# Attention scores for 1024 queries at a time in a tuned single-core kernel

One change to an already tuned attention kernel is predicted without running it, then measured.

## Chip, cores, metric

One core of a Trainium2 chip. The metric is the device time of one execution in microseconds (us); the median of several runs is quoted. A ratio is the mean time of one kernel's fast runs over the mean of the other's in the same rounds, so it is not quite the ratio of the medians.

## The reference

```python
# q, k, v: (8, 2048, 512) float32
scores = np.matmul(q, k.transpose(0, 2, 1)) / np.sqrt(512)
attn_weights = special.softmax(scores, axis=-1)
return np.matmul(attn_weights, v)
```

## The kernel before

Both products, Q with K and the weights with V, use a scheme of two-by-two blocks that needs seven block products instead of eight, paid for with sums of blocks. The sums of K, Q, V and of the weights (the exponentials) are made by VectorE in 16 bits. Scores are made for `QTW` = 512 queries at a time; a matmul of the scores has 256 moving columns:

```python
    QTW = 512
    QH = QTW // 2          # 256 moving columns
    ...
    def product(self, n):  # class Group: one of the seven products, two key blocks (G = 2)
        ...
            for j in range(G):
                for c in range(2):
                    nc.tensor.matmul(
                        dst[:, j * QH:(j + 1) * QH], lhs[:, j, c, :], rhs[:, :, c, :],
                        start=(n in (1, 5) and j == 0 and c == 0), stop=(c == 1),
                        skip_group_check=True,
                    )
```

While TensorE makes the scores of one group of queries, it multiplies the weights of the group before by V, in turn: a slot is one score product, and every other slot has eight matmuls of weights and V after it.

Nothing can be reused from an earlier group at the start. So the first group's scores are made plainly (eight block products), while pieces of K, Q and V (512 rows each, K0 to K3 and so on) come in by casting loads on the GpSimd queue. The scores need K and Q transposed. In the first batch TensorE does this for all of K and for Q0 and Q1; a DMA transpose on the sync queue does it for Q2 and Q3, and for all later batches. The order of the first loads, and a small copy that holds back what follows:

```python
    load("k", 0, 1, (2, 2))
    load("k", 0, 2)
    load("k", 0, 3, room=spare[:, 0])
    load("q", 0, 1, room=spare[:, 1])
    new_v(0)
    for c in range(NCH):
        load_v(0, c)
    load("q", 0, 2, room=spare[:, 2])
    load("q", 0, 3, room=spare[:, 3])
    ...
            if what[0] == "newv":
                if g == 1:     # GpSimd reads transposed Q3: its later loads start after that
                    nc.gpsimd.tensor_copy(out=gate[:], in_=qT[0, 3][0][:, 0, 0, 0:1])
                new_v(bb)
```

The softmax here doesn't subtract the row's maximum and nothing guards it: scores larger than these inputs give would overflow.

Of the kernel before, what the change touches and what calls it, by code (L numbers as in the profile page):

```python
# [12 lines left out]
def kernel(  # L13
# [26 lines left out]
    EXP = mybir.ActivationFunctionType.Exp  # L40
    MULT = mybir.AluOpType.mult
# [4 lines left out]
    QTW = 512  # L46
    NQS = QTW // P
    NQT = T // QTW
# [4 lines left out]
    QH = QTW // 2  # L53
    VP = D + 8
    TP = H + 8
    inv_sqrt_d = float(1.0 / np.sqrt(D))

    G = 2
    NG = NJ // G
    COPY = mybir.ActivationFunctionType.Copy  # L60

    const = ctx.enter_context(tc.tile_pool(name="const", bufs=1))
    stage = ctx.enter_context(tc.tile_pool(name="stage", bufs=4))
    kpool = ctx.enter_context(tc.tile_pool(name="kpool", bufs=5))
    qpool = ctx.enter_context(tc.tile_pool(name="qpool", bufs=3))
    vpool = ctx.enter_context(tc.tile_pool(name="vpool", bufs=2))
    ppool = ctx.enter_context(tc.tile_pool(name="ppool", bufs=2))
    opool = ctx.enter_context(tc.tile_pool(name="opool", bufs=4))
# [18 lines left out]
    qT, kT = {}, {}  # L87
    staged = {}
    vs = {}
# [33 lines left out]
    def operands(what):  # L123
        pool = kpool if what == "k" else qpool
        raw = pool.tile([P, CH, ND, P], F16, tag=what + "raw")
        sums = [pool.tile([P, 2, 2, P], F16, tag=what + f"s{n}", name=what + f"s{n}") for n in (1, 2, 4)]
        return [raw] + sums

    def dma_transpose(what, b, c):
        src = staged.pop((what, b, c))  # L130
        t = operands(what)
        nc.sync.dma_start_transpose(
            out=t[0][:].rearrange("p n c r -> p (n c) r"),
            in_=src[:].rearrange("p n d -> p (n d)"),
        )
        (kT if what == "k" else qT)[b, c] = t

    def transposed(what, b, c, n, src, w, copy):
        if n == 0:
            (kT if what == "k" else qT)[b, c] = operands(what)  # L140
        t = (kT if what == "k" else qT)[b, c]
        tr = psum["px"].tile([P, 2, ND, P], F16, tag="px", name="tr")
        for m in range(w):
            for dc in range(ND):
                nc.tensor.transpose(  # L145
                    tr[:, m, dc, :], src[:, n + m, dc * P:(dc + 1) * P], ident[:]
                )
        copy(out=t[0][:, n:n + w], in_=tr[:, 0:w])

    def pe_transpose(what, b, c, n0=0, n1=CH):  # L150
        src = staged[what, b, c]
        for n in range(n0, n1, 2):
            transposed(what, b, c, n, src, 2, nc.scalar.copy if n else nc.vector.tensor_copy)
        if n1 == CH:
            staged.pop((what, b, c))

    def first_transpose(what, n):
        transposed(what, 0, 0, n, staged[what, 0, 0], 1, nc.vector.tensor_copy)

    def k_blocks(t):  # L160
        w = t[0][:].rearrange("p (j s) c r -> p j s c r", s=2)
        return w[:, :, 0, 0:2], w[:, :, 0, 2:4], w[:, :, 1, 0:2], w[:, :, 1, 2:4]

    def q_blocks(t):
        w = t[0]
        return w[:, 0:2, 0:2], w[:, 2:4, 0:2], w[:, 0:2, 2:4], w[:, 2:4, 2:4]
# [3 lines left out]
    def k_sums(b, c):  # L170
        t = kT[b, c]
        a11, a12, a21, a22 = k_blocks(t)
        _, s1, s2, s4 = t
# [7 lines left out]
    def q_sums(b, c):  # L181
        t = qT[b, c]
        b11, b12, b21, b22 = q_blocks(t)
        _, t1, t2, t4 = t
        return [
            lambda: sub(t1[:], b12, b11),
            lambda: sub(b12, b22, b12),  # L187
            lambda: sub(t2[:], b22, t1[:]),
            lambda: sub(t4[:], b21, t2[:]),
        ]  # L190

    def new_v(b):
        vh = vpool.tile([P, NJ, 2, VP], F16, tag="vh")
        t1 = vpool.tile([P, NJ, TP], F16, tag="t1")
        t2 = vpool.tile([P, NJ, H], F16, tag="t2")
        t4 = vpool.tile([P, NJ, H], F16, tag="t4")
        nc.gpsimd.memset(vh[:, :, 1, D:D + 1], 1.0)
        nc.gpsimd.memset(t1[:, :, H:H + 1], 1.0)
        vs[b] = (vh, t1, t2, t4)

    def load_v(b, c):
        dst = vs[b][0][:].rearrange("p j s d -> p (j s) d")
# [3 lines left out]
    def v_sums(b, c):  # L206
        vh, t1, t2, t4 = vs[b]
# [4 lines left out]
            lambda: sub(t1[:, js, 0:H], b12, b11),  # L212
            lambda: sub(b12, b22, b12),
            lambda: sub(t2[:, js], b22, t1[:, js, 0:H]),
            lambda: sub(t4[:, js], b21, t2[:, js]),  # L215
        ]

    def new_p(g):
        left = [ppool.tile([P, NJ, QH], F16, tag=f"left{s}", name=f"left{s}") for s in range(2)]
        right = ppool.tile([P, NJ, 2, QH], F16, tag="right")  # L220
        sums = [ppool.tile([P, NJ, QH], F16, tag=f"s{n}", name=f"s{n}") for n in (1, 2, 4)]
        pts[g] = (left, right, sums)
# [4 lines left out]
    def plain_tile(g, kb):  # L227

        b, qt = divmod(g, NQT)
        if kb == 0:  # L230
            new_p(g)
        st = bank("qz" if kb % 3 == 2 else "qx")
        c, n = divmod(kb, CH)
        for dc in range(ND):
            nc.tensor.matmul(  # L235
                st[:], kT[b, c][0][:, n, dc, :], qT[b, qt][0][:, :, dc, :],
                start=(dc == 0), stop=(dc == ND - 1),
            )
        left, right, _ = pts[g]
        exp(left[kb % 2][:, kb // 2, :], st[:, 0:QH])  # L240
        exp(right[:, kb // 2, kb % 2, :], st[:, QH:QTW])

    def plain_half(g, j, half):

        b, qt = divmod(g, NQT)
        if j == 0 and half == 0:
            new_p(g)
        st = bank("qx")
        kt, qt_ = kT[b, j // G][0], qT[b, qt][0]
        for s in range(2):  # L250
            for dc in range(ND):
                nc.tensor.matmul(
                    st[:, s * QH:(s + 1) * QH], kt[:, 2 * (j % G) + s, dc, :],
                    qt_[:, 2 * half:2 * half + 2, dc, :],
                    start=(s == 0 and dc == 0), stop=(dc == ND - 1), skip_group_check=True,
                )
        left, right, _ = pts[g]
        if half:
            exp(right[:, j], st[:].rearrange("p (s q) -> p s q", s=2))
        else:  # L260
            for s in range(2):
                exp(left[s][:, j, :], st[:, s * QH:(s + 1) * QH])

    class Group:


        def __init__(self, g, n):
            self.g, self.n = g, n
            self.js = slice(n * G, (n + 1) * G)
            b, qt = divmod(g, NQT)  # L270
            self.a, self.b = kT[b, n], qT[b, qt]

        def product(self, n):
            a11, a12, a21, a22 = k_blocks(self.a)
            b11, b12, b21, b22 = q_blocks(self.b)
            _, s1, s2, s4 = self.a
            _, t1, t2, t4 = self.b
            if n == 1:
                if self.n == 0:
                    new_p(self.g)  # L280
                self.left, self.right, _ = pts[self.g]
# [13 lines left out]
            for j in range(G):  # L295
                for c in range(2):
                    nc.tensor.matmul(  # L297
                        dst[:, j * QH:(j + 1) * QH], lhs[:, j, c, :], rhs[:, :, c, :],
                        start=(n in (1, 5) and j == 0 and c == 0), stop=(c == 1),
                        skip_group_check=True,  # L300
                    )
            getattr(self, f"after{n}", lambda: None)()

        def two(self, t):
            return t[:].rearrange("p (j q) -> p j q", j=G)

# [5 lines left out]
        def after5(self):  # L312
            self.cz = czpool.tile([P, G, 2, QH], F32, tag="cz")
            nc.scalar.copy(out=self.cz[:, :, 1, :], in_=self.two(self.z))  # L314

        def after6(self):
            nc.scalar.copy(out=self.cz[:, :, 0, :], in_=self.two(self.x))  # L317

        def after7(self):
            nc.vector.tensor_add(self.cz[:, :, 1, :], self.two(self.x), self.cz[:, :, 1, :])  # L320

        def after3(self):
            nc.vector.tensor_add(self.cz[:, :, 0, :], self.two(self.z), self.cz[:, :, 0, :])  # L323

        def after4(self):
            exp(self.left[1][:, self.js, :], self.two(self.x))

        def after2(self):
            exp(self.left[0][:, self.js, :], self.two(self.y))

        def exp_right(self):
            exp(self.right[:, self.js], self.cz[:])

    def p_sums(g, n):
        left, right, (s1, s2, s4) = pts[g]
        js = slice(n * G, (n + 1) * G)
        a11, a21 = left[0][:, js], right[:, js, 0]
        a12, a22 = left[1][:, js], right[:, js, 1]
# [6 lines left out]

    class Pair:
# [3 lines left out]
        def __init__(self, g, i):  # L350
            self.g, self.i, self.done = g, i, 0

        def product(self, n):
            g, i = self.g, self.i
            left, right, (s1, s2, s4) = pts[g]
            vh, t1, t2, t4 = vs[g // NQT]
            cols = slice(i * P, (i + 1) * P)
            self.apart = g == NP - 1 and i == 1
            own = "q" if self.apart else "p"
# [4 lines left out]
            elif n == 5:  # L364
# [4 lines left out]
                3: (lambda j: s4[:, j, cols], lambda j: vh[:, j, 1, H:D + 1], "z"),  # L369
                4: (lambda j: right[:, j, 1, cols], lambda j: t4[:, j, :], "x"),  # L370
                5: (lambda j: s1[:, j, cols], lambda j: t1[:, j, 0:H + 1], "z"),
                6: (lambda j: s2[:, j, cols], lambda j: t2[:, j, :], "x"),
# [22 lines left out]
        def store(self, o, half, ds=slice(0, D)):  # L395
            b, qt = divmod(self.g, NQT)
# [273 lines left out]
```

## Time and profile before

| | before |
|---|---|
| median of 3 runs | 806.75 us (806.2 to 807.15) |
| span of the profiled run | 805.1 us |
| TensorE matmuls / weight loads busy | 99% / 88% |
| VectorE / ScalarE busy | 73% / 71% |
| granted TensorE clock | 1.0 throughout |

The prediction shows the lines behind this table and reads them. Matmuls overlap in the trace, so their cost is read from start to start, not from their drawn length.

These are the DMA issues between 0 and 70 us (what, queue, operation and count, then the median from issue to landing in us):

```profile
raw<-vh SPq DMA_TRANSPOSE x2, 4.6
raw<-stage SPq DMA_TRANSPOSE x1, 10.1
```

The two transposes of the first batch landed 4.4 and 4.8 us after their issue (4.6 is the median). The third, at 60 us, took 10.1.

### The profile page before, as it was taken

The page shows a single profiled execution, that of the slowest core. Times are in us where ns is not written, and L with a number is a line of the kernel's source. Part 1 is how long each engine was busy: PE and PEld are TensorE (multiplying, and loading weights), DVE is VectorE, ACT ScalarE, POOL GpSimd, SP SyncE. Part 2 cuts the span into 40 slices and gives each one's busy share as a digit, 9 for nine tenths or more (in the row PEclk, how much of TensorE's full clock was granted, in tenths as well). Part 3 has the DMA queues.
Part 4 walks back from the last instruction along what each step waited for, and adds up shares of the span by engine and source line. Part 5 has one row for each costly group of instructions (what it writes and reads, how often), then busy time and mean ns, then how long its engine had stood idle before and what let it go on. Part 6 is the DMA issues. An engine that isn't in the chain of part 4 may idle for free.

```text
span 805.1 us, 18445 instructions
## 1 busy us (share of the span) xinstructions
PE 798.2 (99%) x7244; PEld 705.1 (88%) x7244; DVE 591.4 (73%) x1477; ACT 571.1 (71%) x1039; POOL 72.7 (9%) x117
## 2 busy tenths in 40 slices
PE   8999999999999999999999999999999999999998
PEld 5788888888888888888888888888888888888887
DVE  4977787787767778677777777777777777766653
ACT  5767767767767777677677677677777776776773
POOL 4020103000030000300002000110002001000000
PEclk9999999999999999999999999999999999999999
DMA  9999966989379992998829997299972998921112
GB/s 207 202 182 179 166 129 116 209 151 183 92 125 216 153 173 70 155 219 142 154 79 162 208 152 154 64 183 197 172 142 67 189 198 158 156 69 46 54 40 79
DMA packets 190246, 116.56 MB, mean 145 GB/s; under 512 B 124496, under 2 KB 172880, under 8 KB 190160
## 3 DMA queue, kind: packets, MB, share of 16 engines
q0 software_dynamic: 49648, 49.29, 39.5%
q1 hardware_dynamic: 140368, 66.08, 39.3%
q8 instruction: 56, 0.92, 0.5%
q14 instruction: 30, 0.25, 0.1%
q10 hardware_dynamic: 144, 0.03, 0.0%
HBM read 100.70 MB, written 33.55 MB: 167 GB/s over the span
## 4 chain that ended last, share of the span: by engine, by line
PE 96%; DVE 2%; DMA 2%; POOL 0%; ACT 0%; issue 0%; SPq 0%; DVEq 0%
PE t L380 48%; PE t L297 46%; DMA stage<-in_k_dram 1%; PE t L235 1%; DMA first<-in_q_dram 1%; PE tr L145 0%; POOL stage L107 0%; DVE t L215 0%; DVE o L391 0%; DVE cz L323 0%; DVE right L342 0%; DVE s L340 0%; ACT o L388 0%; DVE raw L187 0%; DVE s L341 0%
## 5 line engine op out<-in xcount | busy, mean ns | idle before, releaser
L297 PEld LDWEIGHTS <-raw 128*128 128x128 f16 x1984 | 194.1, 98 | 23.4 <-issue 0.6
L388 ACT ACTIVATE o<-t,r 128x256 f32<-128x256 f32 x256 | 122.5, 478 | 128.6 <-DVE r L408 105.7
L297 PE MATMUL t<-raw 128*128 128x256 f16 x1488 | 203.0, 273 | 0.0
L225 ACT ACTIVATE left<-t 128x512 f16<-128x512 f32 (+1 forms) x264 | 156.8, 595 | 21.4 <-PE t L297 18.9
L380 PEld LDWEIGHTS <-s 128*128 128x128 f16 x1536 | 150.3, 98 | 18.5 <-issue 0.2
L297 PEld LDWEIGHTS <-ks 128*128 128x128 f16 x1488 | 145.6, 98 | 17.9 <-issue 0.8
L391 DVE SCALAR_TENSOR_TENSOR o<-t,r,o 128x256 f32<-128x256 f32 x192 | 92.4, 482 | 81.3 <-PE t L380 48.3
L297 PE MATMUL t<-qs,ks 128*128 128x256 f16 x992 | 139.0, 273 | 0.5 <-ACT t L310 0.4
L225 ACT ACTIVATE right<-cz 128x1024 f16<-128x1024 f32 x124 | 132.7, 1070 | 1.5 <-DVE cz L320 1.5
L380 PE MATMUL t<-t,s 128*128 128x257 f16 (+1 forms) x1024 | 133.1, 273 | 0.0
L380 PE MATMUL t<-vh,left 128*128 128x256 f16 x1024 | 132.7, 273 | 0.0
L314 ACT COPY cz<-t 128x512 f32<-128x512 f32 x124 | 72.8, 587 | 67.3 <-PE t L297 67.3
L380 PEld LDWEIGHTS <-right 128*128 128x128 f16 x1024 | 100.2, 98 | 12.2 <-issue 0.6
L320 DVE TENSOR_TENSOR cz<-t,cz 128x512 f32<-128x512 f32 x124 | 85.2, 687 | 34.6 <-PE t L297 34.6
L380 PEld LDWEIGHTS <-left 128*128 128x128 f16 x1024 | 100.2, 98 | 11.6
L323 DVE TENSOR_TENSOR cz<-t,cz 128x512 f32<-128x512 f32 x124 | 84.8, 684 | 1.9 <-PE t L297 1.9
L297 PE MATMUL t<-qs,raw 128*128 128x256 f16 x496 | 74.4, 273 | 0.5 <-DVE cz L320 0.5
L297 PE MATMUL t<-raw,ks 128*128 128x256 f16 x496 | 74.4, 273 | 0.0
L340 DVE TENSOR_TENSOR s<-right 128x512 f16<-128x512 f16 x128 | 54.0, 422 | 27.2 <-ACT right L225 22.2
L317 ACT COPY cz<-t 128x512 f32<-128x512 f32 x124 | 73.2, 591 | 0.2 <-PE t L297 0.2
L310 ACT COPY t<-t 128x512 f32<-128x512 f32 x124 | 70.7, 570 | 3.3 <-ACT o L388 0.3
L380 PE MATMUL t<-vh,s 128*128 128x257 f16 x512 | 66.7, 273 | 0.0
(51 smaller groups left out, 614.1 us busy)
## 6 DMA issues: line engine op xcount, KB each, us to landing
out_dram<-o SPq DMA_DIRECT2D x127, 256.0 KB, 2.8
vh<-in_v_dram POOLq DMA_DIRECT2D x32, 512.0 KB, 14.9
stage<-in_k_dram POOLq DMA_DIRECT2D x29, 512.0 KB, 8.5
stage<-in_q_dram POOLq DMA_DIRECT2D x28, 512.0 KB, 10.3
vh<-in_q_dram POOLq DMA_DIRECT2D x3, 512.0 KB, 20.3
raw<-stage SPq DMA_TRANSPOSE x56, 6.5
first<-in_q_dram SPq DMA_DIRECT2D x2, 256.0 KB, 3.6
first<-in_k_dram SPq DMA_DIRECT2D x2, 256.0 KB, 3.8
```

Of the source, the lines that this page charges most:

```text
L225: nc.scalar.activation(out=out_, in_=in_, func=EXP, scale=inv_sqrt_d)
L235: nc.tensor.matmul(st[:], kT[b, c][0][:, n, dc, :], qT[b, qt][0][:, :, dc, :], start=(dc == 0), stop=(dc == ND - 1),)
L297: nc.tensor.matmul(dst[:, j * QH:(j + 1) * QH], lhs[:, j, c, :], rhs[:, :, c, :], start=(n in (1, 5) and j == 0 and c == 0), stop=(c == 1) ...
L310: nc.scalar.copy(out=self.y[:], in_=self.x[:])
L314: nc.scalar.copy(out=self.cz[:, :, 1, :], in_=self.two(self.z))
L317: nc.scalar.copy(out=self.cz[:, :, 0, :], in_=self.two(self.x))
L320: nc.vector.tensor_add(self.cz[:, :, 1, :], self.two(self.x), self.cz[:, :, 1, :])
L323: nc.vector.tensor_add(self.cz[:, :, 0, :], self.two(self.z), self.cz[:, :, 0, :])
L340: lambda: add(s1[:, js], a21, a22),
L380: nc.tensor.matmul(dst[:, 0:width], lhs(j), rhs(j), start=(first and j == 0), stop=(j == NJ - 1), skip_group_check=True,)
L388: nc.scalar.activation(out=out_, in_=src, func=COPY, scale=r[:])
L391: nc.vector.scalar_tensor_tensor(out=out_, in0=src, scalar=r[:], in1=out_, op0=MULT, op1=ADD)
```

## The change

The intent is fewer and wider matmuls, and less room and work for sums. Scores are made for 1024 queries together, with 512 moving columns. The sums of the weights are made for 128 query pairs when needed, 1024 elements at a time. One fixed set of sums serves K, Q and V instead of rotating buffers. The first plain group is now 1024 queries long, so K3 is wanted some 10 us later (at 33.5 us instead of about 23.5). K3, Q2 and Q3 now go by DMA transpose; V is loaded last; the gate is gone.

```diff
-    QTW = 512
+    QH = 512
+    QW = 2 * QH
 ...
-            for j in range(G):
-                for c in range(2):
-                    nc.tensor.matmul(
-                        dst[:, j * QH:(j + 1) * QH], lhs[:, j, c, :], rhs[:, :, c, :],
+            for dc in range(2):
+                nc.tensor.matmul(
+                    dst[:], lhs[:, j, dc, :], rhs[:, :, dc, :],
 ...
-    kpool = ctx.enter_context(tc.tile_pool(name="kpool", bufs=5))
-    qpool = ctx.enter_context(tc.tile_pool(name="qpool", bufs=3))
-    vpool = ctx.enter_context(tc.tile_pool(name="vpool", bufs=2))
+    spool = ctx.enter_context(tc.tile_pool(name="spool", bufs=2))
 ...   (fixed tiles kraw, ks, qraw, qs, vh, vt1, vt2, vt4)
-            if what[0] == "newv":
-                if g == 1:
-                    nc.gpsimd.tensor_copy(out=gate[:], in_=qT[0, 3][0][:, 0, 0, 0:1])
-                new_v(bb)
 ...
     load("k", 0, 1, (2, 2))
-    load("k", 0, 2)
-    load("k", 0, 3, room=spare[:, 0])
-    load("q", 0, 1, room=spare[:, 1])
-    ...
+    load("q", 0, 1, room=spare[:, 0])
 ...
+    load("k", 0, 2)
+    load("k", 0, 3, room=spare[:, 1])
+    load("q", 0, 2, room=spare[:, 2])
+    load("q", 0, 3, room=spare[:, 3])
+    for c in range(NCH):
+        load_v(0, c)
+    plain_quarter(1, 0)
+    pe_transpose("k", 1, 0, 2)
+    plain_quarter(1, 1)
+    dma_transpose("k", 0, 3)
+    dma_transpose("q", 0, 2)
+    dma_transpose("q", 0, 3)
```

## The prediction

> **What bounds the kernel now.** I read the page first (busy shares, the row of the granted clock, the chain), then the windows of the steady part, then what TensorE itself waits for, then the chain of the first 60 us in order of time, and last the groups of VectorE by form. Page, parts 1, 2 and 4:
>
> ```profile
> PE 798.2 (99%) x7244; PEld 705.1 (88%) x7244; DVE 591.4 (73%) x1477; ACT 571.1 (71%) x1039; POOL 72.7 (9%) x117
> ...
> PEclk9999999999999999999999999999999999999999
> ...
> PE 96%; DVE 2%; DMA 2%; POOL 0%; ACT 0%; issue 0%; SPq 0%; DVEq 0%
> ```
>
> Full clock throughout, and 96% of the chain is TensorE, so the question is how far apart matmuls start, not how long each is drawn in the trace. Windows of the steady part look alike (window, length, busy time and count of PE, PEld, DVE, ACT, POOL, then clock and DMA):
>
> ```profile
> 100.00:200.00 100.00, 100.00 (x918) 89.54 (x916) 77.73 (x195) 72.42 (x131) 9.06 (x14) 1.00 0.88 157
> 600.00:700.00 100.00, 100.00 (x917) 89.54 (x916) 75.80 (x190) 72.74 (x133) 9.82 (x15) 1.00 0.92 158
> ```
>
> The chain gives the spacing from start to start (start, length, what), of the 512-column form in the first two lines, and of the 256-column form in the others:
>
> ```profile
> 17.55 3.45 PE t L235 x16
> ...
> 21.89 2.59 PE t L235 x12
> ...
> 36.68 1.31 PE t L297 x12
> ...
> 129.53 0.88 PE t L380 x8
> 141.77 0.88 PE t L380 x8
> 154.01 0.88 PE t L380 x8
> ```
>
> 512 columns: 3.45/16 = 215.6 ns and 2.59/12 = 215.8, so 215.7. 256 columns: 1.31/12 = 109.2. The last three lines lie 12.24 us apart, half a group of queries, which holds 56 score and 56 weight matmuls (16 of them of 257 columns): 12.24/112 = 109.3, the same. The slope is (215.7 - 109.2)/256 = 0.416 ns a column, which leaves 2.7 ns fixed per matmul. The waits of TensorE in the whole run:
>
> ```profile
> PE t L548 <- DVE warm L512: 1.2, 1, 1.2
> PE t L297 <- DVE cz L320: 0.5, 1, 0.5
> PE t L297 <- ACT t L310: 0.4, 1, 0.4
> ```
>
> The list has three more, of 0.2 to 0.3 us, all in the first 17 us. From 60 us to 780 us TensorE never waits. What is lost lies at the two ends. Windows of TensorE alone (length, busy, count, clock, DMA):
>
> ```profile
> 27.79:40.00 12.21, 11.76 (x104) 1.00 1.23 200
> 40.00:60.00 20.00, 19.41 (x177) 1.00 0.97 181
> 60.00:80.00 20.00, 20.00 (x186) 1.00 1.05 174
> ```
>
> A full 20 us counts 186 (matmuls cut by an edge count too); 40 to 60 us lacks 9 and the stretch before it 10, together about 2 us.
>
> **What the Trainium skill says.** "TensorE: Matmul & The Clock Gate", section "Wait — 56ns, not 53.3ns?": a warm matmul of N columns takes N/2.4 ns plus a fixed 2.5 ns or so, 215.7 ns at 512 columns. The trace agrees: 215.7, and 2.7 fixed. The same page, section "Back-to-back issue gap", gives a sustained 131 ns for 512 columns; 215.7 in this trace contradicts it, and I use the trace. Had it been true, the change would be worth 1680 x 0.085 = 140 us more.
> "Perfetto Trace Analysis", section "Identifying the Most-Contended Engine", says to judge by weight-load busy time instead of matmul busy time. Weight loads are 88% busy at 98 ns each, under the 109.2 ns of a matmul, and nothing waits for them; so fewer loads bring nothing by themselves here.
> "VectorE: DVE Perf Modes", section "The perf-mode tier table", has tensor_tensor on 16-bit data in SBUF at two elements a cycle. The f16 sums of 512 elements here take 0.42 us, spaced 0.33 to 0.34 us in the chain. 512 elements more would cost 512/2/0.96 = 267 ns (an estimate from that page), so a sum of 1024 is about 0.69 us, spaced 0.60.
>
> **The change part by part.** Counts are from listing both kernels' instructions; both build, and the changed one is free of races.
> - Score products (seven instead of eight): 3472 matmuls of 256 columns become 1680 of 512. 1680 x 0.2157 = 362.4 us against 3472 x 0.1092 = 379.1: -16.7 us. (Their columns fall by 28,672, because the first block, made the plain way, is now 1024 queries instead of 512.)
> - Plain scores at the start: 112 matmuls of 512 instead of 48 (the 32 of 256 stay): +64 x 0.2157 = +13.8 us.
> - TensorE transposes at the start: 80 instead of 96; sixteen took 0.89 us in the chain: -0.9 us. The sixteen that are gone (K's last piece of the first batch) go by DMA.
> - Products of weights and V: 2560 + 1024 matmuls in both kernels: 0.
> Sum on TensorE: -16.7 + 13.8 - 0.9 = -3.8 us. As a check: 2048 columns more (+0.85 us) and 1744 matmuls fewer at 2.7 ns (-4.7 us) give the same.
> - VectorE: sums of weights 512 of 512 elements become 192 of 1024, 64 of 768 and 64 of 256; Q sums 124 of 512 become 60 of 1024; score additions 248 become 240 at 0.69 us. By the durations above: 512 x 0.42 - (192 x 0.69 + 64 x 0.56 + 64 x 0.29) = 28, 124 x 0.42 - 60 x 0.69 = 11, and 5 us: busy 591 to about 548. ScalarE: 12 copies at 0.58 and some exponentials fewer, 571 to about 562. Neither is on the path, so worth nothing directly.
> - Weight loads: 5500 instead of 7244, 88% to 67% busy. Worth nothing either.
> - Single sums of K, Q and V: each must be rewritten between its last use and its first use in the next batch. K and Q have four slots or more (a slot is one score product, plus eight weight products in every other: 0.43 or 1.31 us). V is tight: 16 sums of 512 stand in 21 slots at the head of each batch.
>
> **The tight place, by hand.** In those 21 slots TensorE needs 21 x 0.431 + 10 x 0.873 = 17.8 us. VectorE has there, at the spacing in the trace: 16 V sums x 0.34 = 5.4; 6 score additions x 0.60 = 3.6; weight sums 6 x 0.60 + 4 x 0.21 = 4.4; one Q sum 0.6; five output additions x 0.40 and the reciprocals = 2.3. Together 16.3 us, 92%. Following the order of the queue, the V sums end about when their products want them: the last ones of the in-place difference and of the last sum have from none to -0.2 us of slack. I put 0 to 0.3 us a batch, seven batches: 0.7 us.
>
> **The start.** The loads of the first batch land one after the other, 2.65 us a piece (page: about 205 GB/s), K1 at 13.8, V3 at 32 us, well before V's first use at 32.1 (no wait was shown). The changed kernel puts V last: ten pieces end at 37.5, plus three DMA transposes that take about 2.25 us of transfer each (two and one load took 7.1 us at the end of the first phase), so V3 lands at 42 to 44.5. The plain phase ends at 13.8 + 24.2 + 2.2 (transposes) + 0.5 = 40.7, and V is wanted three to four us later: about 0 to 1 us of wait. Against that, VectorE is less crowded there, so some of the 2 us that are lost before 60 us should come back. I take 0 for the two together, plus or minus 1.5.
>
> Total: 806.75 - 3.8 + 0.7 + 0 = 803.65, say 803.7 us.
>
> **Rivals.**
> - Wide matmuls hide weight loads better and so gain much. For: 88% busy loads. Against: a spacing that the columns explain to 2.7 ns, with no waits. It would make 660 to 790 us; 1%.
> - VectorE becomes the bound at the head of each batch. For: 92% in that stretch, where the weight sums are longer and block the additions that free score banks. Against: 73% on average, falling to 68%. At 1 us a batch it makes 810; at 3 us, 824.
> - Transfers: single buffers delay the loads of K, transposes wait on the last reader, and the queue of the stores stands behind them; four output buffers would then hold up ScalarE. For: three staging buffers instead of four, and DMA 80 to 100% busy already. Against: K and Q sums are wanted five us or more after I estimate them in place. It would make 806 to 815.
> - The first phase waits longer for V or Q: 806 to 809.
>
> **Range and chances.** The arithmetic part is sure to some 0.3 us; the waits can hardly fall by over 2 us and can grow by 4. So 801.2 to 808.0. Over 2% faster would be below 790.6, less than the columns allow: 1%. Over 2% slower would be above 822.9, half a us lost in each of 32 query groups: 3%. Within 2%: 96%.
>
> **What would show it.** The matmul count 7244 to 5500, with 512-column matmuls 215.7 apart; TensorE still 98 to 99% busy; weight loads near 67%, VectorE near 548 us; the waits of TensorE short, those for V sums or weight sums at most 0.3 us at each batch head; plain scores ending near 41 us. Wrong would be a steady window whose columns do not fill its time, or a first phase over 2 us longer than reckoned.

## The result, and the profile after

The changed kernel took 820.68 us (818.58 to 821.16, 4 runs) against 806.68 us for the kernel before in the same rounds: ratio 1.017, 95% interval 1.015 to 1.019. The time is above the predicted range (801.2 to 808.0), and in the wrong direction. By the 2% mark it counts as the same; the loss of 14 us is nonetheless clear of noise.

The page, parts 1 and 2:

```profile
PE 799.8 (98%) x5500; PEld 536.0 (66%) x5500; DVE 547.1 (67%) x1212; ACT 570.9 (70%) x1020; POOL 71.6 (9%) x103
...
PEclk9979999999999999999999999999999999999999
```

Counts and busy times are as predicted (5500 matmuls, weight loads 67%, VectorE 548 us); only ScalarE, put at 562, is off. What was not expected is the 7 in the clock row, in the third slice of 20 us. The three longest waits of TensorE for what another engine or a transfer had to finish:

```profile
PE t L227 <- DMA kraw<-vh: 5.8, 1, 5.8
PE t L278 <- DMA qraw<-vh: 2.0, 1, 2.0
PE t L278 <- DVE qs L191: 2.0, 1, 2.0
```

All three are new: K3 transposed, Q2 transposed, then the first sum of Q, which needs Q3 transposed. Where they fall and what the clock does, by windows (length, busy and count of PE, clock, DMA):

```profile
36.00:39.00 3.00, 0.00 (x0) 0.90 1.22 196
39.00:42.00 3.00, 2.77 (x7) 0.50 1.22 197
42.00:45.00 3.00, 3.00 (x8) 0.50 1.48 163
45.00:48.00 3.00, 3.00 (x14) 0.96 1.11 178
...
54.00:57.00 3.00, 3.00 (x9) 0.50 0.99 132
57.00:60.00 3.00, 3.00 (x17) 0.68 1.17 184
60.00:63.00 3.00, 2.87 (x20) 1.00 0.55 90
```

With each spell of waiting the clock goes to half for about 7 us; PE looks fully busy and does half the matmuls (8 of 512 columns in 3 us, not 14). The timeline of TensorE gives the sizes (start, length, what):

```profile
39.23 10.04 PE L227 MATMUL t<-qraw,kraw 128*128 128x512 f16 x32 [5.78 <-DMA kraw<-vh]
51.27 0.60 PE L278 MATMUL t<-qraw,kraw 128*128 128x512 f16 x2 [2.00 <-DMA qraw<-vh]
53.86 1.89 PE L278 MATMUL t<-qs,ks 128*128 128x512 f16 x4 [1.99 <-DVE qs L191]
...
60.53 0.59 PE L278 MATMUL t<-qraw,kraw 128*128 128x512 f16 x2
```

From 39.23 to 51.27 us stand 32 plain matmuls and a wait of 2.0; at 215.7 ns the matmuls need 6.9 of these 12.0 us: 3.1 us lost. From 51.27 to 60.53 us stand 12 matmuls of 512 and 16 of 256 columns, 4.3 us of work, in 9.3 us, of which 2.0 are the wait: 2.9 us lost. With the waits, 5.8 + 2.0 + 2.0 + 3.1 + 2.9 = 15.8 us. The profiled run took 818.58 us; less 15.8 that is 802.8, and the prediction without its V term was 803.0. So nearly the whole miss lies before 60 us, and the rest of the kernel does what was reckoned. (The profiled run is the fastest of the four. The median lies 2.1 us above it, and no kept trace shows where.) The chain in the steady part confirms it, first before, then after:

```profile
125.17 0.87 PE t L297 x8
126.04 0.87 PE t L380 x8
```

```profile
125.23 0.86 PE t L278 x4
126.09 0.87 PE t L373 x8
```

Four score matmuls of 512 columns replace eight of 256, at 0.86 us instead of 0.87.

Why did the transposes land so late? DMA issues of the first 60 us (median from issue to landing):

```profile
qraw<-vh SPq DMA_TRANSPOSE x2, 19.2
kraw<-vh SPq DMA_TRANSPOSE x1, 18.1
```

K3 took 18.1 us, where those of the first batch took 4.4 and 4.8 in the kernel before. The 19.2 is the median of two unlike times: Q2 took 27.6 us and Q3 10.7. All three are issued in turn on the sync queue, and the chain of the first 70 us (start, length, what) shows it:

```profile
23.62 18.60 SPq L143
...
42.31 10.71 DMA qraw<-vh
...
53.11 0.70 DVE qs L191
```

The instruction that issues Q2's transpose lasted 18.6 us, past the landing of K3 (39.2 us), so Q3's was issued at 42.3 only. Q2 landed at 51.2 and Q3 at 53.0, 1.8 us apart, once the loads had run out at 50.7. So the crowd holds each transpose, and the queue puts them one behind the other. The packet records of the trace, counted for each 5 us over the 16 engines of transfer (starts; mean time of a packet on its engine):

```
from us   load packets, 1 KB landing   transpose packets, 256 B
20        1007, 98 ns                  none
25         768, 96 ns                  753, 31 ns
30         759, 96 ns                  786, 31 ns
35         767, 96 ns                  754, 31 ns
```

One to one: it looks as if an engine takes one packet of each queue in turn, so that a transpose packet of 31 ns waits for a load packet of 96. A transpose has 2048 packets, 128 for each engine: 128 x (96 + 31) ns = 16.3 us, the figure that the expectations below use. Packets overlap in the trace, however, as matmuls do. The counts give one transpose packet in about 105 ns on each engine; K3's went from 25.0 to 38.3 us, 13.3 us, and 3.9 us passed between the issue and the first packet. So 16.3 comes near the 18.1 only because two errors partly cancel. Nearly alone, the 2048 packets need 2.0 to 2.7 us (kernel before and e1_gate_v); the kernel before started its transposes at 34.6 us when only the load of Q3 was left.

The Trainium skill has this rule: "DMA: Bandwidth & Descriptors", section "Queues, rings and completion order", says that each transfer engine goes round the queues it has work for, packet by packet. The trace agrees in the counts (753 to 786 of each in 5 us). The page's packet is a group of descriptors, though, and whether a record of the trace is such a group is not shown. The page was not consulted before the prediction.

**Theory.** The loss comes from the crowd in the first 50 us: three DMA transposes, one behind the other, beside up to seven loads (four of V, and three of the second batch, which nothing holds back now). **Rivals:** the transposes are slow whatever runs beside them; the low clock is a loss of its own; the waits add up one by one; the steady part (V sums, single buffers) loses too.

### The profile page after: what moved, and what is told of

It is laid out like the page before. It is cut to its first block, busy times and chain, and to the rows that moved or that the text cites. A ratio compares the mean times of both kernels' runs of the same rounds, so it can differ in the third digit from the quotient of the medians.

```text
span 816.4 us, 14479 instructions
## 1 busy us (share of the span) xinstructions
PE 799.8 (98%) x5500; PEld 536.0 (66%) x5500; DVE 547.1 (67%) x1212; ACT 570.9 (70%) x1020; POOL 71.6 (9%) x103
## 4 chain that ended last, share of the span: by engine, by line
PE 92%; DMA 3%; SPq 2%; DVE 1%; ACT 0%; POOL 0%; issue 0%; DVEq 0%
PE t L373 48%; PE t L278 44%; SPq L143 2%; DMA vh<-in_q_dram 2%; DMA qraw<-vh 1%; DMA first<-in_k_dram 1%; DVE vt L208 0%; SPq L128 0%; ACT o L381 0%; POOL stage L118 0%; POOL vh L118 0%; DVE qs L191 0%; DVE qs L192 0%; DVE cz L301 0%; PE tr L153 0%
## 5 line engine op out<-in xcount | busy, mean ns | idle before, releaser
L278 PE MATMUL t<-qraw,kraw 128*128 128x512 f16 x720 | 195.1, 380 | 2.0 <-DMA qraw<-vh 2.0
L384 DVE SCALAR_TENSOR_TENSOR o<-t,r,o 128x256 f32<-128x256 f32 x192 | 92.3, 481 | 108.6 <-PE t L373 50.7
L278 PEld LDWEIGHTS <-kraw 128*128 128x128 f16 x960 | 94.0, 98 | 64.8 <-DMA qraw<-vh 2.5
L278 PE MATMUL t<-qs,ks 128*128 128x512 f16 x480 | 133.8, 381 | 2.0 <-DVE qs L191 2.0
L373 PE MATMUL t<-vt,s 128*128 128x257 f16 (+1 forms) x1024 | 133.2, 273 | 0.1
L220 ACT ACTIVATE right<-cz 128x1024 f16<-128x1024 f32 x120 | 127.3, 1061 | 1.1 <-DVE cz L298 1.1
L292 ACT COPY cz<-t 128x512 f32<-128x512 f32 x120 | 70.3, 586 | 75.0 <-PE t L278 74.5
L278 PEld LDWEIGHTS <-ks 128*128 128x128 f16 x720 | 70.5, 98 | 49.8 <-DVE qs L191 2.5
L278 PE MATMUL t<-qraw,ks 128*128 128x512 f16 x240 | 71.8, 381 | 0.0
L278 PE MATMUL t<-qs,kraw 128*128 128x512 f16 x240 | 71.4, 379 | 0.0
L295 ACT COPY cz<-t 128x512 f32<-128x512 f32 x120 | 69.8, 582 | 0.3 <-PE t L278 0.3
L373 PE MATMUL t<-vt,right 128*128 128x256 f16 x512 | 67.2, 272 | 0.0
## 6 DMA issues: line engine op xcount, KB each, us to landing
vh<-in_v_dram POOLq DMA_DIRECT2D x32, 512.0 KB, 10.7
```

Of the source, the lines that this page charges most:

```text
L220: nc.scalar.activation(out=out_, in_=in_, func=EXP, scale=inv_sqrt_d)
L278: nc.tensor.matmul(dst[:], lhs[:, j, dc, :], rhs[:, :, dc, :], start=(n in (1, 5) and dc == 0), stop=(dc == 1), skip_group_check=True,)
L292: nc.scalar.copy(out=self.cz[:, 1, :], in_=self.z[:])
L295: nc.scalar.copy(out=self.cz[:, 0, :], in_=self.x[:])
L373: nc.tensor.matmul(dst[:, 0:width], lhs(j), rhs(j), start=(first and j == 0), stop=(j == NJ - 1), skip_group_check=True,)
L384: nc.vector.scalar_tensor_tensor(out=out_, in0=src, scalar=r[:], in1=out_, op0=MULT, op1=ADD)
```

## The experiments

Each is the changed kernel with the edit shown, unless said otherwise. The kernel before ran in the same rounds: 807.2 us in the first four experiments, 807.3 in the next four, 807.6 in the last two. The changed kernel's 820.68 is from its own rounds (with 806.68 beside it), so differences from it carry about 0.6 us of that drift. All ten gave correct results.

### e2_pe_all: no DMA transposes in the first batch

```diff
-    dma_transpose("k", 0, 3)
-    dma_transpose("q", 0, 2)
-    dma_transpose("q", 0, 3)
 ...
+        if (kb, half) == (9, 1):
+            pe_transpose("k", 3)
+        if (kb, half) == (11, 1):
+            pe_transpose("q", 2)
+        if (kb, half) == (12, 1):
+            pe_transpose("q", 3)
```

> The changed kernel with the three DMA transposes of the first batch done on TensorE instead (48 transposes of 128x128 at 55.6 ns, 2.7 us more of TensorE). Theory (crowding): no wait for kraw or qraw is left, the clock stays full, and the time is the arithmetic sum of the prediction without its V term, 803.0, plus 2.7: 805 to 807 us. Rival (the loss comes from the steady part, from V sums or the single buffers): the time stays above 815 us.

Measured: 806.14 us (805.82 to 806.68), ratio to before 0.999 (0.998 to 1.000). Its waits of TensorE, but for the 1.2 us at the very start that all these kernels have:

```profile
PE tr L153 <- DVE qraw L156: 0.5, 2, 0.3
PE t L240 <- DVE kraw L156: 0.4, 1, 0.4
PE t L278 <- ACT t L288: 0.3, 1, 0.3
```

That is all, and the clock is 1.0. The 14 us are gone although every steady part of the change is still there, single sums of V included. The rival of the steady part falls, and the arithmetic (803.0 + 2.7 = 805.7) holds to half a microsecond. Against the kernel before the time is the same within the noise.

### e1_gate_v: V's loads wait for the transposes

```diff
-    for c in range(NCH):
-        load_v(0, c)
     plain_quarter(1, 0)
 ...
     dma_transpose("q", 0, 3)
+    nc.gpsimd.tensor_copy(out=gate[:], in_=raw_of("q", 0, 3)[:, 0, 0, 0:1])
+    for c in range(NCH):
+        load_v(0, c)
```

> The changed kernel with the loads of V (and everything after them on that queue) held back until the third DMA transpose of the first batch has landed. Theory (crowding): in the changed kernel the three transposes share the 16 transfer engines with up to seven queued loads, packet for packet, so each takes 16 us and more, and TensorE waits 5.8 + 2.0 + 2.0 us and loses its full clock. With the loads held, the transposes land by about 34 us (some 5 us or less for each once the Q loads are in), the wait for kraw is gone, V lands at about 45 us and costs a new wait of some 2 us before the first weight product: 804 to 807 us in all. Rival (a transpose is slow whatever runs beside it, or three in a row are): the waits for kraw and qraw stay near 6 and 4 us and the time stays near 820 or grows.

Measured: 812.39 us (810.52 to 814.58), ratio 1.007. The DMA issues and the waits of TensorE:

```profile
qraw<-vh SPq DMA_TRANSPOSE x2, 5.4
kraw<-vh SPq DMA_TRANSPOSE x1, 7.2
```

```profile
PE t L373 <- DMA vh<-in_v_dram: 4.5, 3, 2.1
```

The transposes land in 7.2 (K3), 6.5 and 4.3 us (5.4 is the median of these two), and the waits for them are gone. So neither one alone nor three in a row are slow in themselves. The time missed its range: V's last piece arrived at 48.9 us, not 45, since the loads restarted only after a pause; TensorE waited 0.5, 2.1 and 1.9 us in a row, and here too the clock was at half for about 7 us, from 45.6 us.

### e5_gate_next: only the second batch's loads wait

```diff
     dma_transpose("q", 0, 3)
+    nc.gpsimd.tensor_copy(out=gate[:], in_=raw_of("q", 0, 3)[:, 0, 0, 0:1])
```

> The changed kernel with only the loads of the second batch held until the third DMA transpose has landed, as a gate did in the kernel before; the V loads stay where they are. Theory (turns by packet): at 25 us some 1950 load packets are left instead of 3486, 122 for each engine, so the crowd ends at about 40.5 us instead of 50; the first transpose still lands near 39 us and TensorE still waits 5 to 6 us for it, but the other two land at about 46 us instead of 53, before the plain scores end, so the two waits of 2.0 us go: the time falls by 4 to 6 us against the changed kernel, to 815 to 817 us. Rival (V's loads alone are enough crowd): it falls by less than 2 us.

Measured: 813.35 us (811.1 to 813.87), ratio 1.007: 7.3 us less than the changed kernel (8.3 by the two ratios; either is uncertain by some 2 us). The range, 815 to 817, was missed on the good side. The first transpose still landed at 41 us, and the others in time:

```profile
PE t L227 <- DMA kraw<-vh: 6.4, 1, 6.4
...
PE t L278 <- DVE vt L208: 0.3, 1, 0.3
```

So one line, such as the change dropped, accounts for some 7 us. Most of what remains is the wait for K3 beside V's loads, 6.4 us and a spell of half clock after it.

### e4_halves: load packets of half the size

```diff
-        nc.gpsimd.dma_start(out=dst[:, ns, 0:D], in_=srcs["v"][b, :, ns, :])
+        for ds in (slice(0, H), slice(H, D)) if b == 0 else (slice(0, D),):
+            nc.gpsimd.dma_start(out=dst[:, ns, ds], in_=srcs["v"][b, :, ns, ds])
 ...   (the same for the loads of K and Q of the second batch)
```

> The changed kernel with the first batch's V loads and the second batch's loads cut in two by columns, so that each load packet has half the bytes and there are twice as many. Theory (the engines take one packet of each queue in turn; 768 load and 753 to 786 transpose packets were counted in each 5 us from 25 to 40 us): a transpose packet then waits for a load packet of some 50 to 60 ns instead of 96, so the first transpose takes about 128 x 90 ns = 11 us instead of 16, lands near 34 us, the kraw wait falls from 5.8 us to under 2, and the time falls by 4 to 9 us. Rival (the transposes get what is left in bytes, or are held by their own issue on the sync queue): the landing of the first transpose and the time do not move by more than 1 us, or get worse.

Measured: 816.91 us (816.67 to 819.33), ratio 1.013. The packets per 5 us:

```
from us   load packets, 512 B landing   transpose packets, 256 B
30        1179, 59 ns                   1225, 31 ns
35        1193, 59 ns                   1190, 31 ns
```

K3's landing, from the DMA issues, and the wait for it:

```profile
kraw<-vh SPq DMA_TRANSPOSE x1, 13.8
...
PE t L229 <- DMA kraw<-vh: 2.4, 1, 2.4
```

Still one to one, and the transpose's rate rises by 1.6 although the loads move fewer bytes (0.61 MB in 5 us instead of 0.78). K3 landed 13.8 us after its issue instead of 18.1 (4.0 us to its first packet, then 8.7 for 2048 packets, instead of 3.9 and 13.3), and its wait fell from 5.8 to 2.4 us; under 2 was expected. Equal turns by packet are shown, for two sizes of load packet. A split by bytes is not what these counts look like; nor is a fixed pace of the issuing queue, which follows the crowd: the issue of Q2 lasted 11.5 us here, 18.6 in the changed kernel and 5.0 in e1_gate_v. The time fell by 3.8 us only, below the expected 4 to 9: with twice as many load packets the crowd lasts longer (Q3 landed at 54.2 us), and TensorE waited 8.3 us for the Q sum that needs Q3. These waits are those of the profiled run, 819.33, the slowest of the four.

### e8_k3_pe: only K3 on TensorE

```diff
-    dma_transpose("k", 0, 3)
 ...
+        if (kb, half) == (11, 1):
+            pe_transpose("k", 3)
```

> The changed kernel with only K's last piece of the first batch transposed on TensorE; the two Q pieces stay with DMA. The 5.8 us wait for kraw must vanish. Theory (the phase ends when the last of the crowded transposes lands; the waits and the slow clock before that are not additive): with one transpose fewer the last Q piece lands near 47 to 51 us, TensorE waits 6 to 10 us there instead, and the time falls by 3 to 6 us only, to 815 to 818 us. Rival (waits add up): the time falls by the 5.8 us and the 3.0 us of slow clock after it, 8 to 9 us, less 0.9 us of transposes, to 812.5 to 813.5 us.

Measured: 816.21 us (815.64 to 816.49), ratio 1.011: 4.5 us less, within the theory's range. The 5.8 us wait is gone and another has taken its place:

```profile
PE t L278 <- DVE qs L191: 8.8, 1, 8.8
```

The waits do not add up. The start ends when the last crowded transpose (Q3) has landed; taking away an earlier wait moves the waiting to Q3.

### e3_fill: dummy matmuls in the waits

```diff
+        if (kb, half) == (12, 0):
+            idle(26)
         plain_tile(kb, half, "qz" if n % 3 == 2 else "qx")
 ...
     while background:
         background.popleft()()
+    idle(32)
```

> The changed kernel with 26 and 32 dummy matmuls of 512 columns where TensorE waits in the first 60 us; the waits' causes are left as they are. Theory: of the 15 us lost, about 6 us (3.0 in the last 32 plain matmuls, 3.1 after them) are not waiting but matmuls at the lower clock that the granted-clock row shows after the first wait; with the wait filled the clock stays at 1.0 and the time falls by 5 to 7 us, to 813 to 816 us. Rival (the clock loss is hidden under the later waits for qraw and its sums, which end when the transposes land, 51 to 53 us, whatever the clock): only the part after 53 us comes back, the time falls by 2 to 4 us, to 816.5 to 818.5.

Measured: 818.91 us (817.85 to 819.89), ratio 1.015: only 1.8 us less, a smaller gain than either expected, and nearer the rival's. The clock did stay up:

```profile
40.00:60.00 20.00, 18.57 (x90) 1.00 1.19 182
```

So idling causes the low clock. What the clock costs by itself stays open: 1.8 us came back, of about 6 lost at half clock. The 3.1 us before the waits for Q2 and Q3 lie under those waits, which end when the transposes land. Part of the rest was eaten by the filler itself (the last dummies ran until 54.97 us, later than the 53.86 at which the changed kernel got its Q sum), and TensorE then waited 1.5 us for a sum of V, the next thing in line.

### e10_split: the width alone undone

From e2_pe_all, each score matmul cut in two:

```diff
-            for dc in range(2):
-                nc.tensor.matmul(
-                    dst[:], lhs[:, j, dc, :], rhs[:, :, dc, :],
-                    start=(n in (1, 5) and dc == 0), stop=(dc == 1),
+            for h in range(2):
+                for dc in range(2):
+                    nc.tensor.matmul(
+                        dst[:, h * 256:(h + 1) * 256], lhs[:, j, dc, :], rhs[:, 2 * h:2 * h + 2, dc, :],
+                        start=(n in (1, 5) and h == 0 and dc == 0), stop=(dc == 1),
```

> The version with all first-batch transposes on TensorE (806.1 us), with every score matmul of 512 columns cut into two of 256: the width of the change alone is undone, all else stays. Theory of the prediction (2.7 ns fixed per matmul, weight loads hidden): 1680 matmuls more, 1680 x (2 x 109.2 - 215.7) = 4.5 us slower, 810 to 811.5 us. Rival (width is worth nothing): within 1 us. Rival (the wide form also hides weight loads or waits): slower by over 8 us.

Measured: 810.26 us (809.33 to 812.5), ratio 1.0038 (1.0024 to 1.0052), against 0.9990 for e2_pe_all. The difference of the ratios is 0.48%, 3.9 us, uncertain by some 1.5; 4.5 were reckoned. That is what 512 columns are worth here: a fixed few nanoseconds on 1680 matmuls. TensorE was as free of waits as before (0.3 us at most after 17 us), so no wait and no weight load was hidden by the width.

### e6_one_dma: one transpose back on DMA

From e2_pe_all, with Q3 loaded before K3 and transposed by DMA:

```diff
+    load("q", 0, 3, room=spare[:, 3])
     load("k", 0, 3, room=spare[:, 1])
     load("q", 0, 2, room=spare[:, 2])
-    load("q", 0, 3, room=spare[:, 3])
 ...
+    dma_transpose("q", 0, 3)
 ...
-        if (kb, half) == (12, 1):
-            pe_transpose("q", 3)
```

> A try for a version that beats both: all first-batch transposes on TensorE but the last Q piece's, which goes by DMA and whose load is moved ahead of K's last and Q's third piece. By turns of packets that single transpose takes 128 x 127 ns = 16.3 us beside the loads, from about 22 to 38.5 us, before it is wanted at about 42 us. So no wait, and 16 x 55.6 ns = 0.9 us less than with all on TensorE: 804.5 to 806 us, 0.1 to 0.3% under the kernel before. Rival: it lands after 42 us and costs 1 us or more of wait: 807 us or more.

Measured: 806.94 us (805.8 to 808.92, 6 runs), ratio 0.9993 (0.998 to 1.0007): the range was missed. The transpose landed 18.8 us after its issue at 20.0 us, in time, as the turns by packet say, but the median shows nothing of the 0.9 us saved and lies 1.6 us above the sum. Its profiled run, the fastest at 805.8, had a new wait, of 1.0 us, on ScalarE (whose output tile also waits for a store). Why the runs spread over 3 us is not settled. One source of spread shows in the twelve kept traces: the first score matmul of 512 columns, which waits for the first loads, starts between 12.85 us (this run) and 15.38 us (e10_split), although those loads are nearly the same in all.

### e9_best and e2b_again: a version from the findings

Q2 and Q3 load before K3 and go by DMA transpose with V held back (as in e1_gate_v), K3 goes through TensorE, and the first weight product stands four slots later:

```diff
-    load("k", 0, 3, room=spare[:, 1])
     load("q", 0, 2, room=spare[:, 2])
     load("q", 0, 3, room=spare[:, 3])
-    for c in range(NCH):
-        load_v(0, c)
+    load("k", 0, 3, room=spare[:, 1])
 ...
-    dma_transpose("k", 0, 3)
     dma_transpose("q", 0, 2)
     dma_transpose("q", 0, 3)
+    nc.gpsimd.tensor_copy(out=gate[:], in_=raw_of("q", 0, 3)[:, 0, 0, 0:1])
+    for c in range(NCH):
+        load_v(0, c)
 ...
+        if (kb, half) == (11, 1):
+            pe_transpose("k", 3)
 ...
-        return {2 * n + (5 if g == 0 else 1): x for n, x in enumerate(order)}
+        if g == 0:
+            return dict(zip([9, 11, 13, 16, 17, 18, 19, 21, 23, 25, 26, 27], FIRST))
+        return {2 * n + 1: x for n, x in enumerate(order)}
```

> A version built on the findings: the two Q pieces load before K's last piece and go by DMA transpose with the V loads held until they have landed (so nearly alone on the engines), K's last piece goes through TensorE (16 transposes, 0.9 us), and the first weight product stands four slots (1.7 us) later. Theory: the Q transposes land near 31 to 33 us, V's last piece near 45 us, the first weight product wants it at 45.6 us, no wait is left, and the time is 803.0 + 0.9 = 803.9, that is 803.5 to 805.5 us, 0.2 to 0.4% under the kernel before. Rival: V lands late as in the run with held V loads (48.9 us there), a wait of 2 to 4 us and a spell of low clock: 807 to 810 us.

> The version with all first-batch transposes on TensorE once more, beside the one above on the same chip: 805.5 to 807 us, 0.0 to 0.2% under the kernel before, and 1 to 2 us over the version above if that one has no waits.

Measured: e9_best 804.88 us (803.86 to 806.12), ratio 0.9968 (0.9954 to 0.9982); e2b_again 806.26 us, ratio 0.9984 (0.9972 to 0.9997); before 807.56 us. Both are in their ranges. The transposes of e9_best, and its two longest waits past the start:

```profile
qraw<-vh SPq DMA_TRANSPOSE x2, 6.8
```

```profile
PE t L278 <- DVE cz L298: 0.5, 1, 0.5
PE t L278 <- DVE vt L208: 0.3, 1, 0.3
```

This version beats both kernels, the one before by 0.3%, 2.7 us. That is about what the sums give once the start is in order (-3.8 + 0.9 = -2.9 us).

## Why the prediction was wrong

- **The width.** The -3.8 us on TensorE was right, as far as these runs can tell. Reckoned from the kernel before in the same rounds, e2_pe_all, e2b_again, e9_best and e10_split all land within 0.5 us of sums built on it (e2_pe_all: 807.2 - 3.8 + 2.7 = 806.1, measured 806.14); e6_one_dma lies 1.6 us above its sum. For K3's move to DMA the prediction counted the 0.9 us that TensorE saves and not what it then waits for.
- **The steady part.** The 0.7 us for V sums were not spent; in e2_pe_all TensorE waits for nothing between 60 us and the last stretch. The rival of VectorE was rightly held unlikely.
- **The start: the step that failed.** The prediction took "three DMA transposes that take about 2.25 us of transfer each", from two transposes that ran nearly alone in the kernel before, and used it only to place V; it never set the landing of K3, Q2 and Q3 against the time at which TensorE wants them. The 2.25 us are right for a transpose alone. Beside queued loads the packets of one took 13.3 us, and its landing came 18 to 19 us after the issue (K3, and the first transpose of e3_fill, e5_gate_next, e6_one_dma and e8_k3_pe), because the engines serve the two queues in equal turns, and the transposes follow one another on theirs. K3 landed at 39.2 us, wanted at 33.5; Q3 at 53, wanted at about 41. The term for the start, put at 0 plus or minus 1.5 us, was worth +15.8 us in the profiled run. Its own sign of being wrong came true: the plain scores ended at 49 us, not "near 41 us".
- **What it left out.** It read the dropped gate nowhere. Without it three loads of the second batch join the crowd; that alone is some 7 us (e5_gate_next). It did not note that the change wants Q3 about 24 us earlier than the kernel before. And it had no term for the clock, which fell to half twice; by e3_fill this adds little, since another wait stands behind it.
- **A misreading.** "V3 at 32 us, well before V's first use at 32.1" leaves 0.1 to 0.2 us, and is no sign of room. Here V's last piece landed at 39.8 us, before the 42 to 44.5 reckoned, and no wait was for V.
- **The rivals.** "The first phase waits longer for V or Q" named the right place and put 806 to 809 on it, a third of the effect at most. The rival on transfers, 806 to 815, named the right resource, but in the steady part and for other reasons. By bytes the reckoning was nearly right: 44.5 us for its ten pieces and three transposes, and 8 us for the three loads that it left out, make 52.5, and the last transpose landed at 53.0. What it had wrong is the order: it let the transposes be served as if they came before the loads of V, and they came last.

## What to carry to other kernels

Before moving work from a compute engine to a transfer, look at what else will be queued on the transfer engines at that hour, and, as here, reckon a small-packet transfer at one packet per packet of its neighbours, not at its time alone. Then set its landing against the time at which the data are wanted. Lines that seem to do nothing, like a copy of one column, may be what keeps a later load out of the way; ask of each removed wait what it kept apart. When waits in a start-up phase are taken away one by one, expect the wait to move to the last thing that lands, and count only the phase's end.

## What the Trainium skill lacked or had wrong

- "DMA: Bandwidth & Descriptors", section "Queues, rings and completion order": the rule of turns by packet is there and fits the counts, but the page has no price for a DMA transpose beside loads. Its 2048 packets of 256 B (31 ns) need 2.0 to 2.7 us nearly alone, 13.3 us beside load packets of 1 KB (96 ns) and 8.7 us beside load packets of 512 B (59 ns); the landing goes from 4.4 us to 18.1 and 13.8 us.
- "TensorE: Matmul & The Clock Gate", section "Back-to-back issue gap": its sustained 131 ns for a matmul of 512 columns is not seen; the traces here show 215.7 ns, which its own formula gives.
- The same page, section "Why this matters for your kernels", asks for no idle gaps over about 3 us. In e1_gate_v shorter gaps were enough: the clock fell at 45.6 us (its mean from 45 to 47 us is 0.65), 1.3 us into a gap of 2.1 us, with two matmuls between this gap and one of 0.5 us before it. Single gaps of 1.5 us in e3_fill left it at 1.00.
- "Perfetto Trace Analysis", section "Identifying the Most-Contended Engine", offers weight-load busy time as a measure of headroom, beside the share of the peak rate. Here it fell from 88% to 66% while the time rose by 14 us; no run showed TensorE held up by weight loads.
